# Narrow attention heads of a hybrid decoder step leave fixed filler places; filler is chained behind value transposes

## Chip, cores and metric

One core of a Trainium2 chip runs the whole program in one launch. The metric is device time in microseconds (us), from the first to the last instruction and the little around them; it is taken as the median of several runs. Engines: PE (TensorE, the matmuls), PEld (its weight loads), DVE (VectorE), ACT (ScalarE), POOL (GpSimd), SP (the queue that issues most DMAs).

## What is computed

One step of a decoder with two layers, for a prompt of 1024 tokens and for 8 sample tokens that each have 512 past tokens in a paged cache. Everything is float32 at the interface.

```python
def _diff_attn(q1, q2, q_pos, k1, k2, v, k_pos, table, lam):
    def probs(q, k):
        s = jnp.einsum('bqhd,bkhd->bhqk', q, k).astype(jnp.float32) * scale + bias
        return jax.nn.softmax(jnp.where(mask, s, NEG), axis=-1)
    p = probs(q1, k1) - lam * probs(q2, k2)
    return jnp.einsum('bhqk,bkhe->bqhe', p.astype(v.dtype), v)
...
for layer in range(DEPTH):
    h = _rmsnorm(x, norm_mix[layer])
    # even layer: 4 heads of _diff_attn and 4 of HGRN2; odd layer: 8 heads of _fox_attn and 4 of mLSTM
    x = x + y
    h = _rmsnorm(x, norm_mlp[layer])
    x = x + jnp.square(jax.nn.relu(h @ w_up[layer])) @ w_down[layer]
```

`_fox_attn` is causal attention with one softmax for each head and a forget bias in place of the relative-position bias. In this document "diff" is the attention of layer 0 and "fox" that of layer 1.

## The kernel before

Activations lie transposed (features on partitions, tokens along the free axis). The tokens are cut into two halves: half 0 holds 512 tokens, half 1 the other 512 and the 8 samples. Every projection and MLP matmul splits both operands into two float32r parts and adds three products (high by high, high by low, low by high). `wsplit` (L100 to L109) loads a block of weights and splits it: a DMA on SP, a copy on ACT (L107), a subtraction on POOL (L108). `mm3_parts` (L126) issues the matmuls, all of them on L141, 24 for each split block of the up projection.

The order of the work: projections of layer 0 and HGRN2 of half 0; diff heads of half 0 (here **narrow**: at most 512 keys); diff heads of half 1 (**wide**: up to 1024 keys); HGRN2 of half 1 with the samples' recurrence and attention; then the same for layer 1 with fox heads and mLSTM. Dense work that depends on nothing at hand is **filler**: Python generators in `self.fill` (projections that are still due, then `half` (L1410): the output projection and the MLP of a half that is ready). `tick(n)` (L184) adds rate times n to a credit and takes pieces of filler from the generators until it is used up; a piece of 4096 columns is one unit. `half` first does the part that needs no attention, then says "wait" until the heads of its half are in `heads_done`. At the end of each layer `drain("fill")` issues all that is left.

All four stages of attention run through `attend` (L592). It gets groups (two blocks of 128 query rows) and pipelines them by hand: while the transposes (`prob_t`, L654) and the value matmuls (`pv`, L669) of one group are issued, the scores (L586, L589) of the group 1 or 2 ahead are put between them, with a `tick` at each pair of key blocks. While `attend` runs, `self.chain` is true, and `mm3_parts` ties each piece of filler behind `self.after`, the last score, transpose or value matmul (L140: `issue_after`); so filler keeps the place where it was written. Elsewhere the framework's scheduler (a list scheduler that orders by readiness) puts filler where it sees fit.

For one group: score matmuls into a PSUM tile S; a minimum and the bias on DVE (L632, L634), exp on ACT (L636), the factors and the sum of two maps on DVE (L725, L727); transposes of the probabilities on PE into tile pm (L654); the split into a high part on ACT (L642, Ph) and a low part on DVE (L643, Pl); the value matmuls (L669) into po. The values themselves are transposed on PE and split on ACT and DVE, in chunks of four 128-blocks: `diff_values` (L692, L694, L695) and `fox_values` (L1263, L1267, L1268); each chunk ends with `tick(0.8)`. Wide stages have one PSUM tile pm and two S, narrow ones two pm and three S.

In the sample attention (`diff_sample` L858, `fox_sample` L1341) the probability of the sample's own token goes through DRAM: POOL writes it to `ps_a` or `ps_c`, `sample_out` (L906) reads it back on POOL's queue (L914, L912) into tile pse, multiplies it on DVE (L915) by the own value and adds it to the page values.

```python
    def diff_values(self, vt, u, hd, ps):
...
            nc.vector.tensor_tensor(Vl[:, c0:c0 + 4, :], p3, raw(Vh[:, c0:c0 + 4, :]), op=ALU.subtract)
            self.tick(0.8)
```

Of the kernel before, what the change touches and what calls it, by code (L numbers as in the profile page):

```python
# [19 lines left out]
NP = 1024  # L20
# [44 lines left out]
class Step:  # L65
# [526 lines left out]
    def attend(self, groups, depth, lead, gap):  # L592
# [91 lines left out]
    def diff_values(self, vt, u, hd, ps):  # L684
        nc = self.nc
        n = 4 * (u + 1)
        Vh = hd.tile([128, n, 128], F32R, name="Vh", tag="Vh", bufs=2)
        Vl = hd.tile([128, n, 128], F32R, name="Vl", tag="Vl", bufs=2)
        for c0 in range(0, n, 4):
            pt = ps.tile([128, 512], F32, name="pm", tag="m")  # L690
            for c in range(4):
                nc.tensor.transpose(pt[:, 128 * c:128 * c + 128], vt[:, 128 * (c0 + c):128 * (c0 + c + 1)], self.ident[:])  # L692
# [3 lines left out]
            self.tick(0.8)  # L696
        return Vh, Vl

    def diff_half(self, u, hd, pm, pS, need=()):

        nc = self.nc
        W = 512 * (u + 1)
        parts, vt, V, po, P, es, st = {}, {}, {}, {}, {}, {}, {}

        def prep(h, g):
            if g == 2 * u:
                if need:
                    self.drain("fill", need[h])
                parts[h] = self.diff_parts(h, u, hd)
                if h == 0:  # L710
                    vt[0] = self.values(self.O["va"][0:128, :], u, hd)

        def score(h, i, m):
# [5 lines left out]
            es[m] = hd.tile([128, W], F32, name="e", tag="e", bufs=5 if u else 7)  # L719
# [10 lines left out]
        def tr(h, g, j):  # L730
            if h == j == 0 and g == 2 * u:
                V[0] = self.diff_values(vt[0], u, hd, pm)
            if g == 2 * u and j == 0:
                po[h] = pm.tile([128, 512], F32, name="po", tag="po", bufs=1)
                if h < 3 and not need:
# [7 lines left out]
        def end(h, g):  # L743
            if g == 2 * u:
                if h < 3:
                    if need:
                        vt[h + 1] = self.values(self.O["va"][128 * h + 128:128 * h + 256, :], u, hd)
# [5 lines left out]
            self.tick(2.5 if u else 1.5)  # L753

        groups = []
        for h in range(4):
            for g in (2 * u, 2 * u + 1):
                steps = [lambda h=h, i=i, m=m: score(h, i, m) for i in (2 * g, 2 * g + 1) for m in range(2)]
                groups.append(Group(lambda h=h, g=g: prep(h, g), steps, g + 1, lambda j, h=h, g=g: tr(h, g, j),
                                    lambda j, p, h=h, g=g: pv(h, g, j, p), lambda h=h, g=g: end(h, g), late=u == 1 and g == 2))  # L760
        self.attend(groups, 1 if u else 2, 0 if u else 1, 1.3 if u else 1.0)
# [96 lines left out]
    def diff_sample(self, ph, ps, pS):  # L858
# [47 lines left out]
    def sample_out(self, ph, ov, pself, vs):  # L906
# [6 lines left out]
        else:  # L913
            nc.gpsimd.dma_start(pb[:], pself)  # L914
        nc.vector.tensor_tensor(pb[:], pb[:], vs[:], op=ALU.mult)  # L915
# [339 lines left out]
    def fox_values(self, vt, u, hd, ps):  # L1255
# [4 lines left out]
        for c0 in range(0, n, 4):  # L1260
            pt = ps.tile([128, 512], F32, name="pm", tag="m")
            for c in range(4):
                nc.tensor.transpose(pt[:, 128 * c:128 * c + 128], vt[:, 128 * (c0 + c):128 * (c0 + c + 1)], self.ident[:])  # L1263
# [5 lines left out]
            self.tick(0.8)  # L1269
        return VV  # L1270

    def fox_half(self, u, hd, pm, pS):

        nc, W = self.nc, 512 * (u + 1)
        self.Q2 = [hd.tile([128, 512], F32R, name=f"Q2{r}") for r in range(2)]
        self.K2 = [hd.tile([128, W], F32R, name=f"K2{r}") for r in range(2)]
        for r in range(2):
            nc.gpsimd.memset(raw(self.K2[r][64:128, :]), 0.0)
            nc.gpsimd.memset(raw(self.Q2[r][64:128, :]), 0.0)
            nc.gpsimd.memset(raw(self.Q2[r][64:66, :]), 1.0)  # L1280
# [3 lines left out]
        def prep(h, g):  # L1284
            if g == 2 * u:
# [4 lines left out]
        def score(h, qi):  # L1290
# [3 lines left out]
            e = hd.tile([128, W], F32, name="e", tag="e", bufs=4 if u else 6)  # L1294
# [8 lines left out]
        def tr(h, g, j):  # L1303
            i, r = divmod(h, 2)
            if h == j == 0 and g == 2 * u:
                VV[0] = self.fox_values(vt[0], u, hd, pm)
            if g == 2 * u and j == 0:
# [9 lines left out]
        def end(h, g):  # L1317
            i, r = divmod(h, 2)
            if g == 2 * u + 1:
# [9 lines left out]
        for h in range(8):  # L1329
            for g in (2 * u, 2 * u + 1):  # L1330
                groups.append(Group(lambda h=h, g=g: prep(h, g), [lambda h=h, qi=qi: score(h, qi) for qi in (2 * g, 2 * g + 1)], g + 1,
                                    lambda j, h=h, g=g: tr(h, g, j), lambda j, p, h=h, g=g: pv(h, g, j, p), lambda h=h, g=g: end(h, g)))
        self.attend(groups, 1 if u else 2, 1, 1.3 if u else 1.0)
# [459 lines left out]
```

## Time and profile before

| | |
|---|---|
| runs | 2935.47, 2938.91, 2945.58 us; median 2938.91 us |
| profiled execution | 2948.05 us, span of its instructions 2946.3 us |
| busy | PE 94%, DVE 47%, POOL 39%, ACT 35% of the span |
| granted clock of PE, mean | 0.97 of full |
| stages by the trace | narrow diff 325 to 470 us, wide diff 470 to 640, narrow fox 1232 to 1346, wide fox 1930 to 2200 |

"Idle" is time in which an engine runs nothing; the profile names what ended it (the releaser). [...] Lines are those of the kernel before.

### The profile page before, as it was taken

Reading aid. Unit: us, or ns where it says so; the run is one execution under the profiler, and the core shown is the slowest. Engines: PE = TensorE matmul, PEld = TensorE weight load, DVE = VectorE, ACT = ScalarE, POOL = GpSimd, SP = SyncE. Lnnn points to the kernel's source line nnn. Section 1 sums busy time; section 2 is a strip of 40 time slices with the busy share of each in tenths; the row PEclk is TensorE's granted clock in tenths of the full one; section 3 lists DMA queues with packets and bytes.
Section 4 is the critical chain, followed back from the end, with each engine's and each line's share of the span. In section 5 each row is a group of like instructions: output and inputs, shape, how many; then the busy total and the mean of one; then the engine's idle time right before and its main releaser. Section 6 shows DMA issues by size and latency. Waiting matters only on the chain. (4 is left out here: it accounts for less than half of the span.)

```text
span 2946.3 us, 44581 instructions
## 1 busy us (share of the span) xinstructions
PE 2772.6 (94%) x17410; PEld 2458.7 (83%) x17410; DVE 1375.5 (47%) x2668; ACT 1039.1 (35%) x1741; POOL 1141.5 (39%) x688
## 2 busy tenths in 40 slices
PE   8999898889889989989999989889999999999997
PEld 7999786677678878889999979867777777999997
DVE  5134457665654354374322246365544533532234
ACT  4111346552222232374323332155542223323233
POOL 3323323223843434422344434843323334344443
PEclk9999899899999999999999999989999999999998
DMA  4332444225544354523322244742235333422222
GB/s 141 112 122 80 135 152 128 76 85 163 157 125 151 110 153 151 159 78 111 120 93 88 93 152 129 235 129 85 69 111 164 107 97 103 147 94 91 90 94 73
DMA packets 174685, 349.73 MB, mean 119 GB/s; under 512 B 28914, under 2 KB 67298, under 8 KB 174474
## 3 DMA queue, kind: packets, MB, share of 16 engines
q1 hardware_dynamic: 174250, 346.81, 37.5%
q8 instruction: 137, 2.24, 0.3%
q0 software_dynamic: 224, 0.07, 0.2%
q14 instruction: 74, 0.61, 0.1%
HBM read 297.92 MB, written 48.88 MB: 118 GB/s over the span
## 5 line engine op out<-in xcount | busy, mean ns | idle before, releaser
L108 POOL TENSOR_TENSOR wl<-wr,wh 128x1024 fp32r<-128x1024 f32 (+1 forms) x361 | 866.9, 2402 | 1334.4 <-ACT wh L107 1259.8
L107 ACT ACTIVATE wh<-wr 128x1024 fp32r<-128x1024 f32 (+1 forms) x361 | 381.5, 1057 | 1126.8 <-PE acc L141 908.1
L141 PE MATMUL acc<-uh,wh 128*128 128x260 f32 (+1 forms) x2080 | 674.3, 327 | 25.6 <-DVE ul L1408 10.6
L141 PE MATMUL acc<-ul,wh 128*128 128x260 f32 (+1 forms) x2080 | 666.4, 321 | 3.8 <-DVE ul L1408 2.8
L141 PE MATMUL acc<-xh,wh 128*128 128x260 f32 (+1 forms) x1760 | 590.3, 335 | 15.7 <-ACT xh L238 7.7
L141 PE MATMUL acc<-uh,wl 128*128 128x260 f32 (+1 forms) x1856 | 602.0, 325 | 0.0
L141 PE MATMUL acc<-xl,wh 128*128 128x260 f32 (+1 forms) x1760 | 588.0, 334 | 2.7 <-DVE xl L239 2.6
L141 PE MATMUL acc<-xh,wl 128*128 128x260 f32 (+1 forms) x1760 | 586.1, 333 | 1.1 <-POOL wl L108 1.1
L141 PEld LDWEIGHTS acc<-uh,wh 128*128 128x128 f32 x2080 | 395.4, 191 | 61.1 <-DVE x L1431 10.9
L1431 DVE TENSOR_TENSOR x<-acc,x 128x260 f32<-128x260 f32 (+1 forms) x464 | 238.0, 517 | 402.7 <-PE acc L141 400.8
L141 PEld LDWEIGHTS acc<-ul,wh 128*128 128x128 f32 x2080 | 397.6, 191 | 32.6 <-DVE ul L1408 5.8
L141 PEld LDWEIGHTS acc<-uh,wl 128*128 128x128 f32 x1856 | 354.1, 191 | 28.7 <-issue 0.8
L141 PEld LDWEIGHTS acc<-xh,wh 128*128 128x128 f32 x1760 | 334.3, 190 | 50.8 <-ACT xh L238 8.0
L141 PEld LDWEIGHTS acc<-xl,wh 128*128 128x128 f32 x1760 | 334.8, 190 | 33.3 <-DVE xl L239 3.8
L141 PEld LDWEIGHTS acc<-xh,wl 128*128 128x128 f32 x1760 | 334.8, 190 | 31.6 <-POOL wl L108 1.2
L1405 DVE SCALAR_TENSOR_TENSOR acc<-acc,rb 128x260 f32<-128x260 f32 (+1 forms) x192 | 100.2, 524 | 258.5 <-PE acc L141 257.1
L141 PE MATMUL acc<-ih,wh 128*128 128x260 f32 (+2 forms) x600 | 194.0, 324 | 7.7 <-ACT wh L107 4.8
L141 PE MATMUL acc<-ih,wl 128*128 128x260 f32 (+2 forms) x600 | 192.9, 324 | 4.5 <-POOL wl L108 4.5
L141 PE MATMUL acc<-il,wh 128*128 128x260 f32 (+2 forms) x600 | 192.7, 321 | 0.0
L215 DVE TENSOR_TENSOR z<-acc,rb 128x512 f32<-128x512 f32 (+1 forms) x138 | 69.6, 511 | 259.0 <-PE acc L141 238.2
L1408 DVE TENSOR_TENSOR ul<-acc,uh 128x260 fp32r<-128x260 f32 (+1 forms) x192 | 98.5, 513 | 141.9 <-ACT uh L1407 141.4
L141 PE MATMUL acc<-x,wh 128*128 128x260 f32 x448 | 128.4, 289 | 0.8 <-DVE z L215 0.7
(406 smaller groups left out, 3826.1 us busy)
## 6 DMA issues: line engine op xcount, KB each, us to landing
wr<-in_w_up SPq DMA_DIRECT2D x128, 512.0 KB
wr<-in_w_down SPq DMA_DIRECT2D x128, 512.0 KB
wr<-in_w_in_o SPq DMA_DIRECT2D x48, 512.0 KB
wr<-in_w_out SPq DMA_DIRECT2D x32, 512.0 KB
wr<-in_w_in_e SPq DMA_DIRECT2D x27, 512.0 KB
qd<-qS SPq DMA_DIRECT2D x64, 128.0 KB
dk<-in_cache_k_a SPq DMA_DIRECT2D x32, 256.0 KB
dk<-in_cache_v_a SPq DMA_DIRECT2D x32, 256.0 KB
```

Of the source, the lines that this page charges most:

```text
L107: nc.scalar.activation(h[:, :kk, :m], r[:, :kk, :m], AF.Copy)
L108: nc.gpsimd.tensor_tensor(l[:, :kk, :m], r[:, :kk, :m], raw(h[:, :kk, :m]), op=ALU.subtract)
L141: nc.tensor.matmul(out, lhsT=w[:, k, :m], rhs=a[:, sl], start=(n == 0), stop=(n == last))
L215: nc.vector.tensor_tensor(d, p, r, op=ALU.mult)
L1405: nc.vector.scalar_tensor_tensor(p, p, 0.0, self.rb[u][:, sl], op0=ALU.max, op1=ALU.mult)
L1408: nc.vector.tensor_tensor(L[:, sl], p, raw(H[:, sl]), op=ALU.subtract)
L1431: nc.vector.tensor_tensor(x[f][:, sl], pt[:, :m], x[f][:, sl], op=ALU.add)
```

## The change

The narrow stages (half 0 of both layers) no longer go through `attend`. New functions `diff_head` and `fox_head` write one head after the other, with `self.chain` false; filler is taken by `tick(L / NP)` after each score, at rates of 5.2 and 5.0 in place of 1, and is not tied to a place. The wide stages keep `attend`, with larger ticks in its first part (5 for 4, 1.6 for 0.7). In `diff_values` and `fox_values` the transposes now set `self.after`, and a chunk's tick is 1.3 for 0.8, in the wide stages only. `half` gives up one more unit before its RMS norm. The read of the own probability is written ahead of the page values.

```diff
 def attend(...)
-        self.tick(4)
+        self.tick(5)
         for G in groups[:depth]:
             for step in G.steps:
                 step()
-                self.tick(0.7)
+                self.tick(1.6)
...
 def diff_values(...)          # fox_values the same, with L1302 for L1263
-        Vh = hd.tile([128, n, 128], F32R, name="Vh", tag="Vh", bufs=2)
+        Vh = hd.tile([128, n, 128], F32R, name="Vh", tag="Vh", bufs=u + 1)
...
-                nc.tensor.transpose(pt[:, 128 * c:128 * c + 128], vt[:, 128 * (c0 + c):128 * (c0 + c + 1)], self.ident[:])
+                self.after = nc.tensor.transpose(pt[:, 128 * c:128 * c + 128], vt[:, 128 * (c0 + c):128 * (c0 + c + 1)], self.ident[:]).ins
...
-            self.tick(0.8)
+            if self.chain:
+                self.tick(1.3)
...
+    def diff_head(self, h, hd, ps, pS, parts, nxt):
+        po = ps.tile([128, 512], F32, name="po", tag="po", bufs=1)
+        for g in range(2):
+            P = []
+            for i in (2 * g, 2 * g + 1):
+                st = hd.tile([128, 2, 2], F32, name="st", tag="st", bufs=4)
+                es = []
+                for m in range(2):
+                    S = pS.tile([128, 512], F32, name="S", tag="S")
+                    L = self.scores(S, parts[m], i)
+                    w = min(L, 256)
+                    e = hd.tile([128, 512], F32, name="e", tag="e", bufs=5)
+                    self.soft_neg(S, L, e, st[:, m, :], self.bias[:, h, 256 - w:])
+                    self.tick(L / NP)
+                    es.append(e)
+                if i == 1:
+                    after = nxt()
...
+            if g == 0:
+                Vh, Vl = self.diff_values(self.values(self.O["va"][128 * h:128 * h + 128, :], 0, hd), 0, hd, ps)
+            o = po[:, 256 * g:256 * g + 256]
+            for j in range(g + 1):
+                self.pv(o, g, j, self.prob_t(hd, ps, P, g, j), lambda kb: ((Vh[:, kb, :], 0), (Vh[:, kb, :], 1), (Vl[:, kb, :], 0)))
...
 def diff_sample(...)          # fox_sample the same
         nc.gpsimd.dma_start(pself[:].rearrange("o r -> r o"), p2[:, 512:513])
+        pb = self.own_probs(ph, pself[:].to_broadcast([128, 32]))
         pick = self.row_picker(ph)
         ov = ph.tile([128, 32], F32, name="ov", tag="ov")
         yield from self.page_values(...)
-        o = self.sample_out(ph, ov, pself[:].to_broadcast([128, 32]), self.va_s)
+        o = self.sample_out(ph, ov, pb, self.va_s)
...
 def half(...)
         if not alone:
+            yield 1
             rms()
...
 def run(...)
-                self.fill = (1, self.fill[1] + [self.half(0, 0, accM, accM)])
+                self.fill = (5.2, self.fill[1] + [self.half(0, 0, accM, accM)])
...
-                self.diff_half(0, hd, pm, pS, dp[2::3])
+                self.diff_first(hd, pm, pS, dp[2::3])
...
-                self.fill = (1, self.fill[1])
+                self.fill = ((5.0, 1)[u], self.fill[1])
...
-                    self.fox_half(u, hd, pm, pS)
+                    (self.fox_wide if u else self.fox_first)(hd, pm, pS)
```

`fox_head` is `diff_head` with one map for each row block and the normalisation on DVE or ACT; `diff_first` and `fox_first` call the heads in turn and prepare the next head's queries and keys from inside (`nxt`). Three places in the order of PE show what this moves. Names with numbers are particular buffers; K, Q are the operands of a score, vt and pm the values and the PSUM tile of a transpose, xh, xl, uh, ul and x those of filler.

The first place is PE at the start of the narrow diff heads, where head 0's first scores stand (L586, L589) and the constants of the relative-position bias (L535). Before:

```order
L286 MATMUL hms<-hsq,ones 128x512
L141 MATMUL acc<-uh,wh 128x260
L141 MATMUL acc<-x_186,wl 128x260
L586 MATMUL S<-K_3217,Q_3216 128x128
L589 MATMUL S<-K_3220,Q_3216 128x128
...
L141 MATMUL acc<-x_238,wl 128x260
L535 MATMUL pm<-oh,tb 128x384 x4
L586 MATMUL S<-K_3230,Q_3229 128x256
L589 MATMUL S<-K_3233,Q_3229 128x256
```

And now, at the same place:

```order
L286 MATMUL hms<-hsq,ones 128x512
...
L141 MATMUL acc<-xh_156,wl 128x512
L586 MATMUL S<-K_3217,Q_3216 128x128
L589 MATMUL S<-K_3220,Q_3216 128x128
L141 MATMUL acc<-xh_169,wh 128x512
...
L535 MATMUL pm<-oh,tb 128x384
L141 MATMUL acc<-ul,wh 128x260
L141 MATMUL acc<-x_225,wl 128x260
L141 MATMUL acc<-x_238,wh 128x260
L535 MATMUL pm<-oh,tb 128x384
```

The first scores stand 42 filler matmuls later (36 of 260 columns, 6 of 512), and the four L535, which stood together, have filler between them.

The second place is PE in the wide diff heads, at the second chunk of the third head's values (L692) and the first transposes of probabilities behind it (L654). Before:

```order
L586 MATMUL S<-K_5447,Q_5446 128x384
L589 MATMUL S<-K_5450,Q_5446 128x384
L692 MATMUL pm<-ident,vt 128x128 x4
L654 MATMUL pm<-ident,e 128x128 x4
L141 MATMUL acc<-xh_4690,wh 128x512
L141 MATMUL acc<-xl_4691,wh 128x512
```

Now:

```order
L586 MATMUL S<-K_5532,Q_5531 128x384
L589 MATMUL S<-K_5535,Q_5531 128x384
L692 MATMUL pm<-ident,vt 128x128 x4
L141 MATMUL acc<-uh,wh 128x512
...
L141 MATMUL acc<-uh,wl 128x512
L586 MATMUL S<-K_5545,Q_5544 128x512
L589 MATMUL S<-K_5548,Q_5544 128x512
L586 MATMUL S<-K_5545,Q_5544 128x384
L589 MATMUL S<-K_5548,Q_5544 128x384
L654 MATMUL pm<-ident,e 128x128 x4
```

Twelve filler matmuls and four of scores now stand between L692 and L654, where nothing stood.

The third place is PE at the end of the narrow diff heads: the last head's values (L692), transposes and value matmuls (L669). Now:

```order
L141 MATMUL acc<-uh,wl 128x512
L692 MATMUL pm<-ident,vt 128x128 x4
L654 MATMUL pm<-ident,e 128x128 x7
L669 MATMUL po<-Ph,Vh 128x256
...
L669 MATMUL po<-Pl,Vh 128x256
L654 MATMUL pm<-ident,e 128x128 x3
L669 MATMUL po<-Ph,Vh 128x256 x2
L669 MATMUL po<-Ph,Vl 128x256 x2
L669 MATMUL po<-Pl,Vh 128x256 x2
```

Before, the last head's transposes were:

```order
L286 MATMUL hms<-hsq,ones 128x512
L654 MATMUL pm<-ident,e 128x128 x3
L141 MATMUL acc<-uh,wh 128x512
...
L654 MATMUL pm<-ident,e 128x128 x4
L141 MATMUL acc<-uh,wh 128x512
...
L654 MATMUL pm<-ident,e 128x128 x3
L141 MATMUL acc<-uh,wh 128x512
```

So 32 matmuls of one head now stand in a row; before, 6 to 12 filler matmuls stood behind each of its three groups of transposes.

## Rows read from the trace of the kernel before

**Rows 1.** The page's first line

```profile
span 2946.3 us, 44581 instructions
```

**Rows 2.** Windows by stage: us, busy PE, PEld, DVE, ACT, POOL (instructions), PEclk, DMA share, GB/s

```profile
325.00:470.00 145.00, 129.60 (x719) 108.60 (x718) 78.68 (x205) 68.43 (x151) 43.78 (x34) 0.93 0.50 155
470.00:640.00 170.00, 140.53 (x673) 114.68 (x671) 127.69 (x230) 103.24 (x168) 46.51 (x22) 0.91 0.28 81
1232.00:1346.00 114.00, 102.14 (x752) 96.95 (x752) 87.12 (x192) 80.72 (x189) 33.83 (x23) 0.94 0.39 108
1440.00:1730.00 290.00, 284.07 (x2348) 281.97 (x2346) 95.98 (x209) 95.14 (x161) 117.14 (x49) 1.00 0.32 103
1930.00:2200.00 270.00, 244.39 (x1265) 204.22 (x1263) 159.44 (x245) 147.41 (x248) 86.28 (x46) 0.95 0.30 88
```

**Rows 3.** Waits of PE in 325 to 470 us: us in total, times, longest

```profile
PE S L586 <- ACT e L636: 3.7, 4, 2.0
PE pm L535 <- POOL tb L533: 3.0, 2, 2.6
PE S L586 <- ACT K L563: 2.2, 1, 2.2
PE S L589 <- POOL K L567: 1.3, 2, 1.0
PE pm L535 <- POOL bt L538: 1.0, 1, 1.0
```

**Rows 4.** Waits of PE in 1232 to 1346 us

```profile
PE po L669 <- DVE ft L1322: 4.2, 2, 2.1
PE acc L261 <- DVE sq L251: 2.3, 1, 2.3
```

**Rows 5.** Waits of PE in 470 to 640 us

```profile
PE S L586 <- ACT e L636: 9.3, 11, 3.4
PE pm L654 <- DVE Vl L695: 8.1, 3, 3.3
PE pm L654 <- DVE e L727: 3.2, 1, 3.2
PE po L669 <- DVE Pl L643: 2.6, 3, 1.2
```

**Rows 6.** Waits of PE in 1930 to 2200 us

```profile
PE S L586 <- ACT e L636: 6.8, 4, 4.4
PE pm L654 <- DVE VV L1268: 6.2, 4, 1.9
PE pm L1263 <- DVE VV L1268: 3.7, 2, 2.1
```

**Rows 7.** Windows of line L141 alone: us, PE busy (instructions), PEld, PEclk

```profile
940.00:1040.00 100.00, 97.12 (x411) 76.91 (x411) 1.00 0.39 125
1450.00:1700.00 250.00, 247.39 (x2054) 246.32 (x2053) 1.00 0.27 91
```

**Rows 8.** Timeline of PE, wide diff heads: start, us, what, count, idle before and its releaser

```profile
573.68 0.66 PE L654 MATMUL pm<-ident,e 128*128 128x128 f32 x4 [2.71 <-DVE Vl L695]
...
598.78 0.50 PE L586 MATMUL S<-K,Q 128*128 128x512 f32 x1 [3.41 <-ACT e L636]
```

**Rows 9.** Timeline of POOL, DVE and PE, 846 to 861 us

```profile
852.17 0.57 POOL L914 DMA_DIRECT2D pse<-ps_a  x1 [5.04 <-DMA ps_a<-dp]
...
858.52 0.91 DVE L915 TENSOR_TENSOR pse<-pse,va_s 128x32 f32<-128x32 f32 x1 [8.55 <-DMA pse<-ps_a]
...
860.08 0.79 PE L141 MATMUL acc<-xh,wh 128*128 128x512 f32 x1 [4.84 <-DVE x L1431]
```

**Rows 10.** Timeline of DVE and POOL, 801 to 812 us, and POOL's weight split (part 5)

```profile
801.77 10.42 DVE L394 TENSOR_TENSOR hq<-hq,hpe 128x256 f32<-128x256 f32 x1
...
801.75 4.67 POOL L108 TENSOR_TENSOR wl<-wr,wh 128x1024 fp32r<-128x1024 f32 x2
...
L108 POOL TENSOR_TENSOR wl<-wr,wh 128x1024 fp32r<-128x1024 f32 (+1 forms) x361 | 866.9, 2402 | 1334.4 <-ACT wh L107 1259.8
```

More of the change, by code (lines that the diff above doesn't have):

```diff
@@ L703, in diff_half, with diff_wide @@
+    def diff_wide(self, hd, pm, pS):
+        nc = self.nc
+        W, u = NP, 1
         parts, vt, V, po, P, es, st = {}, {}, {}, {}, {}, {}, {}
         def prep(h, g):
-            if g == 2 * u:
-                if need:
-                    self.drain("fill", need[h])
+            if g == 2:
                 parts[h] = self.diff_parts(h, u, hd)
@@ L1268, in fox_values @@
                 nc.vector.tensor_tensor(d[:, :, 64:128], p3[:, :, 64 * r:64 * r + 64], raw(d[:, :, 0:64]), op=ALU.subtract)
-            self.tick(0.8)
-        return VV
[L1272 to L1280, printed above, removed]
+            if self.chain:
+                self.tick(1.3)
@@ new lines, in fox_values, with fox_head @@
+        return VV
+    def fox_head(self, h, hd, ps, pS, parts, VV, nxt):
+        nc = self.nc
+        i, r = divmod(h, 2)
+        po = ps.tile([128, 512], F32, name="po", tag="po", bufs=1)
+        for g in range(2):
+            if g % 2:
+                after = nxt()
+            P = []
+            for qi in (2 * g, 2 * g + 1):
+                st = hd.tile([128, 2], F32, name="st", tag="st", bufs=4)
+                S = pS.tile([128, 512], F32, name="S", tag="S")
+                L = self.scores(S, parts, qi, mask=True)
+                e = hd.tile([128, 512], F32, name="e", tag="e", bufs=4)
+                self.soft_neg(S, L, e, st)
+                self.tick(L / NP)
+                nc.vector.reciprocal(st[:, 1:2], st[:, 1:2])
+                if r:
+                    nc.scalar.activation(e[:, :L], e[:, :L], AF.Copy, scale=st[:, 1:2])
+                else:
+                    nc.vector.tensor_scalar(e[:, :L], e[:, :L], st[:, 1:2], None, op0=ALU.mult)
+                P.append(e)
+            if h == g == 0:
+                VV = self.fox_values(self.values(self.O["vc"][0:128, :], 0, hd), 0, hd, ps)
+            o = po[:, 256 * g:256 * g + 256]
+            for j in range(g + 1):
+                self.pv(o, g, j, self.prob_t(hd, ps, P, g, j), lambda kb: ((VV[r][:, kb, :], 0), (VV[r][:, kb, :], 1)))
+        t = hd.tile([64, 512], F32, name="ft", tag="ft", bufs=1)
+        nc.scalar.copy(t[:], po[64:128, :])
+        nc.vector.tensor_tensor(t[:], po[0:64, :], t[:], op=ALU.add)
+        nc.sync.dma_start(self.os[1][0][i][64 * r:64 * r + 64, :512], t[:])
+        if r == 1 and i < 3:
+            VV = self.fox_values(self.values(self.O["vc"][128 * i + 128:128 * i + 256, :], 0, hd), 0, hd, ps)
+        return after, VV
@@ L1376, in fox_sample @@
         nc.gpsimd.dma_start(pself[:].rearrange("h (b o) -> (h b) o", o=1), e[:, 512:513])
+        pse = pself[:].rearrange("(i r) b -> r i b", r=2)
+        pb = self.own_probs(ph, tuple(pse[r].unsqueeze(0).to_broadcast([64, 4, NS]) for r in range(2)))
         pick = self.row_picker(ph)
@@ L1387, in fox_sample @@
         yield from self.page_values(ph, ps, I["cache_v_c"], PP, sel, ov)
-        pse = pself[:].rearrange("(i r) b -> r i b", r=2)
-        o = self.sample_out(ph, ov, tuple(pse[r].unsqueeze(0).to_broadcast([64, 4, NS]) for r in range(2)), self.vc_s)
+        o = self.sample_out(ph, ov, pb, self.vc_s)
         nc.sync.dma_start(self.os[1][1][0:4][:, :, 512:].rearrange("i p b -> p i b"), o[:].rearrange("p (i b) -> p i b", b=NS))
@@ L1666, in hgrn_half, with diff_first, nxt, fox_first @@
         self.staggered([self.hgrn_unit(h, u, ph, pm, need.get(h)) for h in range(4)], lag)
+    def diff_first(self, hd, pm, pS, need):
+        def nxt(h):
+            if h == 4:
+                return None
+            self.drain("fill", need[h])
+            return self.diff_parts(h, 0, hd)
+        parts = nxt(0)
+        for h in range(4):
+            parts = self.diff_head(h, hd, pm, pS, parts, lambda: nxt(h + 1))
+    def fox_first(self, hd, pm, pS):
+        self.fox_ones(512, hd)
+        parts, VV = self.fox_parts(0, 0, hd), None
+        for h in range(8):
+            parts, VV = self.fox_head(h, hd, pm, pS, parts, VV, lambda: self.fox_parts(h + 1, 0, hd) if h < 7 else None)
 @with_exitstack
```

70 lines of the change are left out of this document (46 added, 24 removed).

## Prediction, made before the run

> **What bounds the kernel now.** I read the page's busy shares first: PE runs for 94% of the span [rows 1], three products for each matmul, and no other engine is busy for half of it. The time is therefore PE's work plus PE's idle time plus what it loses while the granted clock stands at its lower level. The change removes no matmul, so it can only act on the two losses.
>
> Second, the windows by stage, to see where these losses lie [rows 2]. Idle is a window's length less PE's busy time: 145 - 129.60 = 15.4 us in the narrow diff heads, 29.5 in the wide diff heads, 11.9 in the narrow fox heads, 25.6 in the wide fox heads, together 82.4 us. The clock loss is the length times (1 - PEclk): 10.2, 15.3, 6.8 and 13.5, together 45.8 us. While a layer's left-over filler is drained, in the 290 us behind the narrow fox stage, PE idles 5.9 us and stands at the upper level throughout. So the four stages that the change rewrites hold 128 us of loss, and filler issued in them or in the drain costs the same: 100/411 = 0.243 us for 512 columns, 250/2054 = 0.122 us for 260 [rows 7]. Moving filler gains nothing by itself; it gains when it stands where PE would wait.
>
> Third, PE's waits in each of the four stages, by releaser [rows 3 to 6]. The reader is to see that no single wait is large: the list is of 1 to 4 us waits on ACT's exp, on the values' split, and on POOL's constants.
>
> **The change part by part.** Counts of filler are from the two orders; durations are from the rows.
>
> *Narrow diff heads.* Filler now goes where the scheduler finds it ready, and the first scores stand behind 36 x 0.122 + 6 x 0.243 = 5.9 us more of it. The waits for the first key operands (2.2 and 1.3), for the bias constants tb and bt (3.0 and 1.0) and the longest one of a score for exp (2.0) are each shorter than that [rows 3]: 9.5 us go. Against it, the last head's 32 matmuls stand in a row, where filler covered each of three softmax and split chains before. Such a chain shows as 3.2 us where it is bare (transposes for DVE's e) and 2.71 or 3.3 (for Vl) [rows 5, 8]; I take one of them, 3 us, as the heads ahead still overlap. Sum **-6.5**. Bounds: -9.5 if the tail costs nothing; -0.5 if tb and bt stay (4.0) and the tail costs 5.
>
> *Narrow fox heads.* The 4.2 us for the factor ft (L1322), which sat in front of chained value matmuls, go, since 45 more pieces of filler (5.5 us) now stand in the stage; the wait for the square (2.3) belongs to `half` and stays [rows 4]. The longest stretch without filler grows from 77 to 89 attention matmuls, for which I charge 1 us. Sum **-3.2**, bounds -4.2 and 0.
>
> *Wide diff heads.* Behind a chunk's transposes there are now 12 filler matmuls, 2.9 us, and four scores. They cover the 8.1 us for Vl (three waits, longest 3.3) [rows 5, 8]. The larger tick of the first part covers the 3.2 us for e, whose wait stands near the stage's start. What is late next: the filler used there is missing elsewhere, and at two heads in place of one the first scores come in a burst that outruns exp, as in the 3.41 us wait at 598.78 [rows 8], so +3.4; the longest dry stretch grows from 42 to 50 matmuls, +2. Sum -8.1 - 3.2 + 3.4 + 2 = **-5.9**, bounds -11.3 without the penalties and -0.5 with them doubled. 76 more 512-column matmuls are used in this stage, 18.5 us; they leave the drain.
>
> *Wide fox heads.* The same cover takes the 6.2 us of transposes behind VV; the 3.7 us at L1263, where the next chunk waits for the same buffer, may grow by 2, since there is less filler between chunks; the longest wait for exp, 4.4, falls in the first part, whose ticks more than double [rows 6]. Sum -6.2 + 2 - 4.4 = **-8.6**, bounds -10.6 and -2.2.
>
> *Own probabilities.* At nothing. In the kernel before, POOL already issues this read at 852.17, right behind the write it waits for (5.04 us of idle time there), long before the line that names it would suggest. The multiply on DVE then waits 8.55 us, and PE 4.84 us behind it [rows 9]. The change writes the read ahead, but the multiply keeps its place early in DVE's order, ahead of the evictions that PE needs, so the wait stays. This is the part that may not do what it says. Bounds: -4.8 if the multiply moves, +2 if POOL, whose queue the read holds, delays the row picks behind it.
>
> *The rest.* One more yield ahead of the RMS norm and single-buffered narrow values cost nothing: the wait for the square stays, and the values' loads keep their places in SP's order, so nothing is queued behind a new wait there.
>
> *Clock.* Idle time goes down by 6.5 + 3.2 + 5.9 + 8.6 = 24.2 us. In these stages clock loss is 45.8/82.4 = 0.56 of the idle time [rows 2]. Were it to follow, 13.5 us would go too; not every gap is followed by a stretch at the lower level, so I take half, **-6.7**, with bounds 0 and, at the largest idle gain, 0.56 x 35.6 = 19.9.
>
> *Sum.* 24.2 + 6.7 = 30.9 us off the profiled execution's 2948.05, whose span is 2946.3: 2917.2. The median of the runs shown is 9.1 below that execution, so **2908 us**. All bounds at their best: 35.6 + 19.9 off, 2883; all at their worst: 3.2 off, 2936.
>
> **The rivals.**
>
> *More than forecast.* One subtraction of 256 elements on DVE took 10.42 us, with POOL's weight splits running back to back from the same moment [rows 10]. If the moved filler shifts POOL's splits, this stall may not recur, up to 10.4 us, and the rest of the proportional clock gain comes with it: 2908 - 10.4 - 6.7 = 2891. For it: it is an accident of order, and the order changes. Against: other splits can fall on other DVE work.
>
> *Less than forecast.* The filler moved into attention brings its splits along. 76 and 42 more matmuls of 24 per block are 5 splits on POOL of 2402 ns each [rows 10], 12 us beside DVE's softmax chains. If those are held up by as much and the clock gains nothing, 2908 + 12 + 6.7 = 2927. For it: the same row, which shows DVE held by POOL. Against: most of DVE's softmax reads PSUM, and the mean POOL load of these stages is 27 to 32%. [...]
>
> *Slower.* The narrow heads lose their hand pipelining. If the scheduler lets the first softmax chain of each of the 12 narrow heads stand bare, at 3.2 us [rows 5], that is 38 us, with half the clock's share (0.28 x 38 = 11) 49: 2908 + 49 = 2957. It decides from 10 of the 12 heads on (10 x 4.1 = 41). For it: the dry stretches above, and single-buffered values. Against: the new order puts the next head's scores ahead of the last value matmuls of the one before, mostly with a dozen pieces of filler between.
>
> **How the numbers follow.** About 0.3%, 8.8 us, is what a measurement of this kernel can tell from no change: faster is below 2930.1, slower above 2947.7. The forecast (2896 to 2922) has 0.50, the larger gain 0.14, the smaller gain (2917 to 2938) 0.22, of which half lies below 2930.1, the slower case 0.14. Faster is 0.50 + 0.14 + 0.11 = 0.75, same 0.11, slower 0.14. The range 2883 to 2938 leaves out the slower case and a little of the larger gain.
>
> **What would show it.** Right: PE's waits at L654 for Vl and VV fall below 3 us in each wide stage; the waits for ft, tb and K in the narrow stages are gone; PE is idle under 60 us in the four stages, with PEclk up in all four; the drains are shorter by about 20 us in layer 0; DVE still waits 8 us for pse. Wrong: a new wait of PE for DVE's e or ACT's exp at the start of most narrow heads (the slower case), DVE operations of 5 us or more beside POOL's splits in the wide stages (the smaller gain), or an unchanged PEclk with fewer gaps, which would say that the clock hangs on something other than these waits.

## The result and the profile after

| | before | after |
|---|---|---|
| median of the runs, us | 2940.31 (5 runs, 2935.47 to 2951.26) | 2909.83 (5 runs, 2906.02 to 2919.53) |
| ratio, 95% interval | | 0.9898 [0.9869, 0.9927] |
| profiled execution, us | 2948.05 | 2906.02 |

The kernel became 1.0% faster, 30 us, at 2909.83 us; the forecast was 2908 us. The page of the profile after begins:

```profile
span 2904.3 us, 44586 instructions
...
PE 2757.2 (95%) x17408; PEld 2447.8 (84%) x17410; DVE 1378.9 (47%) x2668; ACT 1038.7 (36%) x1741; POOL 1142.4 (39%) x688
```

PE idles 2904.3 - 2757.2 = 147.1 us, where the profiled execution before had 173.7 (2946.3 - 2772.6). The windows by stage, which answer to [rows 2] (narrow diff, wide diff, narrow fox, the drain behind it, wide fox; same columns; each stage begins and ends where it does before, counted from its first and last scores):

```profile
330.00:460.00 130.00, 120.49 (x695) 101.64 (x694) 83.59 (x204) 68.35 (x150) 44.16 (x34) 0.99 0.54 167
460.00:643.00 183.00, 154.64 (x748) 126.46 (x746) 137.53 (x236) 108.82 (x177) 54.40 (x24) 0.93 0.27 82
1205.00:1319.00 114.00, 102.73 (x800) 98.97 (x799) 89.07 (x198) 80.67 (x191) 37.97 (x26) 0.97 0.39 116
1410.00:1700.00 290.00, 284.52 (x2352) 282.43 (x2350) 96.18 (x209) 94.69 (x161) 118.26 (x54) 1.00 0.33 107
1898.00:2168.00 270.00, 249.89 (x1311) 208.72 (x1311) 160.82 (x247) 150.00 (x250) 90.44 (x48) 0.97 0.31 92
```

Idle time of the four attention stages is 9.5 + 28.4 + 11.3 + 20.1 = 69.3 us (82.4 before) and their clock loss 1.3 + 12.8 + 3.4 + 8.1 = 25.6 us (45.8 before). The wide diff stage is longer because more filler lies in it. PEclk is the mean granted clock of a stretch, as a share of full; the traces of the two kernels show two levels of it, 1.00 (470 to 490 us in the kernel before) and 0.50 (492 to 500). PE's waits in the narrow diff heads ([rows 3] before):

```profile
PE pm L654 <- DVE hrs L291: 2.0, 1, 2.0
...
PE po L669 <- ACT Ph L642: 1.1, 1, 1.1
PE pm L535 <- POOL tb L533: 1.0, 1, 1.0
```

In the narrow fox heads ([rows 4] before):

```profile
PE acc L141 <- DVE x L1512: 4.0, 4, 1.6
PE po L669 <- DVE ft L1341: 3.1, 1, 3.1
PE acc L141 <- DVE ul L1480: 1.6, 1, 1.6
```

In the wide diff heads ([rows 5] before):

```profile
PE S L586 <- ACT e L636: 11.8, 9, 3.6
PE po L669 <- DVE Pl L643: 5.6, 2, 5.3
PE acc L141 <- DVE x L1512: 2.8, 1, 2.8
...
PE pm L654 <- DVE Vl L695: 0.6, 1, 0.6
```

And in the wide fox heads ([rows 6] before; VV is now on L1307, the values' transposes on L1302):

```profile
PE pm L654 <- DVE VV L1307: 8.4, 2, 6.3
PE po L669 <- DVE Pl L643: 3.5, 7, 1.0
PE pm L1302 <- DVE VV L1307: 2.6, 2, 1.6
...
PE S L586 <- ACT e L636: 0.2, 1, 0.2
```

The reader is to see what went as planned (K, most of tb, Vl, exp in the wide fox heads) and the two waits of over 5 us that are new, for Pl (5.3) and for VV (6.3).

### The profile page after: what moved, and what is told of

Read it like the earlier page. It is cut to its first block, busy times and chain, and to the rows that moved or that the text cites. A ratio compares the mean times of both kernels' runs of the same rounds, so it can differ in the third digit from the quotient of the medians.

```text
span 2904.3 us, 44586 instructions
## 1 busy us (share of the span) xinstructions
PE 2757.2 (95%) x17408; PEld 2447.8 (84%) x17410; DVE 1378.9 (47%) x2668; ACT 1038.7 (36%) x1741; POOL 1142.4 (39%) x688
## 5 line engine op out<-in xcount | busy, mean ns | idle before, releaser
L141 PE MATMUL acc<-uh,wh 128*128 128x260 f32 (+1 forms) x2080 | 673.5, 327 | 27.7 <-DVE x L1512 16.0
L141 PE MATMUL acc<-ul,wh 128*128 128x260 f32 (+1 forms) x2080 | 665.5, 321 | 5.9 <-DVE ul L1480 4.6
L141 PE MATMUL acc<-uh,wl 128*128 128x260 f32 (+1 forms) x1856 | 601.5, 325 | 0.0
L141 PE MATMUL acc<-xh,wh 128*128 128x260 f32 (+1 forms) x1760 | 587.3, 334 | 11.4 <-ACT xh L238 8.1
L141 PE MATMUL acc<-xl,wh 128*128 128x260 f32 (+1 forms) x1760 | 585.7, 333 | 2.5 <-DVE xl L239 2.5
L141 PE MATMUL acc<-xh,wl 128*128 128x260 f32 (+1 forms) x1760 | 583.3, 332 | 0.0
L141 PEld LDWEIGHTS acc<-uh,wh 128*128 128x128 f32 x2080 | 394.5, 191 | 67.0 <-DVE x L1512 19.6
L141 PEld LDWEIGHTS acc<-ul,wh 128*128 128x128 f32 x2080 | 396.4, 191 | 36.6 <-DVE ul L1480 7.4
L141 PEld LDWEIGHTS acc<-uh,wl 128*128 128x128 f32 x1856 | 353.4, 190 | 28.4 <-issue 0.7
L141 PEld LDWEIGHTS acc<-xh,wh 128*128 128x128 f32 x1760 | 332.8, 189 | 44.6 <-ACT xh L238 8.1
L141 PEld LDWEIGHTS acc<-xl,wh 128*128 128x128 f32 x1760 | 333.6, 190 | 31.9 <-DVE xl L239 3.4
L141 PEld LDWEIGHTS acc<-xh,wl 128*128 128x128 f32 x1760 | 333.1, 189 | 30.2 <-issue 0.8
L141 PE MATMUL acc<-ih,wh 128*128 128x260 f32 (+2 forms) x600 | 194.8, 325 | 7.3 <-ACT wh L107 5.5
L141 PE MATMUL acc<-ih,wl 128*128 128x260 f32 (+2 forms) x600 | 193.3, 324 | 4.5 <-POOL wl L108 4.5
L141 PE MATMUL acc<-il,wh 128*128 128x260 f32 (+2 forms) x600 | 193.7, 323 | 0.0
L141 PE MATMUL acc<-x,wh 128*128 128x260 f32 x448 | 128.6, 290 | 0.8 <-DVE z L215 0.7
```

Source lines behind the costliest of these rows:

```text
L141: nc.tensor.matmul(out, lhsT=w[:, k, :m], rhs=a[:, sl], start=(n == 0), stop=(n == last))
```

## The experiments

All are compared with the kernel before, run on the same chip beside them. Besides the median, the table splits the time in two, over all executions: **clock loss** is the span times (1 - its mean granted clock), **the rest** is the span without it, which is PE's work at a PEclk of 1.00 plus its idle time. PE's work does not change: in the 14 profiled executions, one of each kernel and a second of the kernel before, the rest less PE's idle time comes to 2680 to 2690 us. So differences of the rest are, to a few us, differences of idle time. The row "before" holds all executions on the three chips of the experiments; by chip its rest is 2852, 2853 and 2851 us and its clock loss 89, 87 and 90. The rest varies little from one execution to the next (standard deviation 1 to 4 us; 7 for f1_kdve_hq).

| kernel | executions | median us | ratio, 95% interval | rest us | clock loss us |
|---|---|---|---|---|---|
| before | 57 | 2940 to 2942 | | 2852 | 89 |
| after | 5 | 2909.83 | 0.9898 [0.9869, 0.9927] | 2831 | 79 |
| e1_narrow | 12 | 2943.03 | 1.0002 [0.9984, 1.0020] | 2841 | 100 |
| e2_wide | 6 | 2918.01 | 0.9916 [0.9888, 0.9944] | 2836 | 80 |
| e3_small | 12 | 2953.28 | 1.0043 [1.0026, 1.0060] | 2853 | 101 |
| e4_hq_pool | 12 | 2940.50 | 0.9983 [0.9964, 1.0001] | 2846 | 91 |
| e5_no_small | 6 | 2909.41 | 0.9894 [0.9873, 0.9914] | 2828 | 81 |
| e6_ticks | 6 | 2922.18 | 0.9935 [0.9920, 0.9950] | 2833 | 88 |
| e7_values | 12 | 2939.27 | 0.9995 [0.9979, 1.0010] | 2847 | 93 |
| e8_kdve | 5 | 2905.89 | 0.9882 [0.9863, 0.9901] | 2828 | 76 |
| f1_kdve_hq | 6 | 2911.28 | 0.9891 [0.9870, 0.9911] | 2828 | 82 |
| f2_spread | 4 | 2907.91 | 0.9876 [0.9856, 0.9896] | 2828 | 80 |
| f3_all | 5 | 2891.94 | 0.9824 [0.9807, 0.9840] | 2814 | 76 |

**e1_narrow**: only the narrow heads are new. Against the changed kernel:

```diff
-        self.tick(5)
+        self.tick(4)
...
-                self.tick(1.6)
+                self.tick(0.7)
...
-                self.after = nc.tensor.transpose(pt[:, 128 * c:128 * c + 128], vt[:, 128 * (c0 + c):128 * (c0 + c + 1)], self.ident[:]).ins
+                nc.tensor.transpose(pt[:, 128 * c:128 * c + 128], vt[:, 128 * (c0 + c):128 * (c0 + c + 1)], self.ident[:])
...
-                self.tick(1.3)
+                self.tick(0.8)
```

and the two small edits of e3_small taken back.

> The changed kernel with its wide stages, own-probability reads and the yield ahead of the RMS norm as before: only the narrow heads are new. Theory A (the gain comes from the waits that each part takes away in its own stages): about 0.4% faster than before (2940), 2928 us (9.7 us of waits and 2.7 of clock), idle time in the wide stages as before (29.5 and 25.6). Theory B (the gain outside the four stages, at the DVE stall of 10.4 us and the wait of 4.8 us for the own probability, comes with any new order): 2915 to 2925 with those two gone from the recurrence of half 1. Theory C (narrow heads lose by giving up their pipeline): slower than 2945.

The time did not move, which none of the three theories gave. The table shows what offset what: the rest fell by 11 us, near theory A's 9.7, and the clock loss rose by 11. The windows of its profile (the four attention stages):

```profile
330.00:458.00 128.00, 121.25 (x696) 102.44 (x695) 83.66 (x203) 66.95 (x148) 42.96 (x34) 0.97 0.54 168
458.00:634.00 176.00, 146.03 (x683) 118.48 (x682) 130.12 (x231) 105.19 (x171) 48.89 (x22) 0.89 0.27 81
1216.00:1330.00 114.00, 103.60 (x798) 99.80 (x797) 90.25 (x197) 80.07 (x190) 37.31 (x23) 0.96 0.39 115
1914.00:2190.00 276.00, 246.56 (x1264) 205.51 (x1264) 158.50 (x245) 148.37 (x248) 86.48 (x46) 0.94 0.28 84
```

The narrow stages idle 6.8 and 10.4 us (15.4 and 11.9 before), so their heads lost nothing by giving up the pipeline: theory C falls. The wide stages, whose code is that of before, idle 30.0 and 29.4 us (29.5 and 25.6 before) and stand at a PEclk of 0.89 and 0.94 (0.91 and 0.95 before). But the clock loss of the four stages together, 44 us, is no larger than before (45.8). In this profile 7 us of the added loss lie elsewhere, in the recurrence of half 1 and in a stretch in which PE never idles. The window, in the kernel before and in e1_narrow:

```profile
700.00:750.00 50.00, 50.00 (x282) 40.72 (x281) 28.60 (x66) 12.19 (x20) 19.79 (x16) 1.00 0.36 111
700.00:750.00 50.00, 50.00 (x251) 40.52 (x250) 26.77 (x60) 10.53 (x19) 17.11 (x15) 0.86 0.32 101
```

PE is busy for 50.00 of 50.00 us in both, and r1_before (below), a second profile of the kernel before, has 1.00 there too. In the 5 us ahead of the fall PE runs only matmuls of the recurrence, most of them of 64 columns and of 1 (L388, L470), with no filler between them. The kernel before has 7 us of such work at 714 us and keeps its clock, so what tips it is not shown.

**e2_wide**: only the wide part, in the kernel before.

```diff
-        self.tick(4)
+        self.tick(5 if depth == 1 else 4)
...
-                self.tick(0.7)
+                self.tick(1.6 if depth == 1 else 0.7)
...
+                self.after = at if u else self.after
...
-            self.tick(0.8)
+            self.tick(1.3 if u else 0.8)
```

> The kernel before with only the wide part: larger ticks in the first part of the pipeline, and filler chained behind the value transposes, in the wide stages alone. Theory A: 2921 us, 0.6% faster (14.5 us of waits and 4 of clock); PE's waits behind Vl and VV under 3 us in each wide stage, the narrow stages as before (15.4 and 11.9 idle). Theory B: in the wide stages new waits (exp, Pl) give back what Vl and VV free, at most 7 us of idle time go there, and what else is gained lies in the recurrence of half 1.

2918 us: most of the whole change's gain, 16 us of the rest and 9 of clock loss, near theory A's 14.5 and 4. In its profile the two wide stages idle 25.5 and 20.0 us (29.5 and 25.6 before), more of a fall than theory B's 7. But not all of it is by theory A's waits: PE waits 1.8 us for Vl, and still 7.4 for VV (L1270).

**e3_small**: only the own probability's read, written earlier, and one more yield.

```diff
+        pb = self.own_probs(ph, pself[:].to_broadcast([128, 32]))
         pick = self.row_picker(ph)
...
         if not alone:
+            yield 1
             rms()
```

> The kernel before with only the own-probability read written earlier and one more yield ahead of the RMS norm. Theory A: no change, 2935 to 2945, PE still waits about 4.8 us behind the own probability. Theory B: the order of the recurrence moves and 5 to 15 us go, 2925 to 2935, in the recurrence of half 1.

0.43% slower, against both theories. The rest is unchanged (2853 against 2852), so in sum no idle time was added or taken. The whole difference is clock loss, 12 us; which of the two edits moves it was not run. The profile holds the stall of hq (9.27 us), DVE's wait for the own probability (8.52) and PE's wait for the eviction behind it (4.84), in two lines of DVE and one of PE:

```profile
812.02 9.27 DVE L394 TENSOR_TENSOR hq<-hq,hpe 128x256 f32<-128x256 f32 x1
...
868.23 0.94 DVE L921 TENSOR_TENSOR pse<-pse,va_s 128x32 f32<-128x32 f32 x1 [8.52 <-DMA pse<-ps_a]
```

```profile
869.83 0.80 PE L141 MATMUL acc<-xh,wh 128*128 128x512 f32 x1 [4.84 <-DVE x L1438]
```

**e4_hq_pool**: the product that stalled in [rows 10], on POOL.

```diff
-            nc.vector.tensor_tensor(Q[:, :, hh:], Q[:, :, hh:], p2[:, :, 0:1].to_broadcast([128, nb, hh]), op=ALU.mult)
+            nc.gpsimd.tensor_tensor(Q[:, :, hh:], Q[:, :, hh:], p2[:, :, 0:1].to_broadcast([128, nb, hh]), op=ALU.mult)
```

> The kernel before with the decayed queries of the recurrence (hq by hpe, L394) multiplied on POOL in place of DVE, so that DVE has no two-input SBUF product there that POOL's own work can hold up. If the 10.4 us stall of that one product is in every execution of the kernel before: about 10 us faster, 2930, with no idle time of PE over 5 us in 780 to 830 us. If it is an accident of the one profiled execution, or POOL's longer queue gives it back: 2935 to 2945.

The time lies in the second range, and the interval of the ratio just touches 1; the rest fell by 6 us. A stall of 10 us in every execution would have given more, if POOL's longer queue gives none of it back, which was not told apart. A second profile of the kernel before, r1_before, with nothing edited:

> The kernel before once more, for a second profile. If its idle time is set by the order of the instructions: 163 to 167 us of idle time on PE again, of it 9 to 11 in one wait behind the product hq (L394) at about 802 us, and the time differs from 2948 by as much as the clock loss differs. If the stall is an accident of one execution: no DVE operation over 5 us, idle time 150 to 155.

Its time was 2946.53 us, its PE busy for 2782.2 of 2944.8 us, so idle for 162.6, 11 less than the first. That is near the first branch's idle time, but without the stall that it names. On DVE and POOL, where the first had the 10.42 us:

```profile
804.79 1.18 DVE L394 TENSOR_TENSOR hq<-hq,hpe 128x256 f32<-128x256 f32 x1
```

```profile
803.32 4.87 POOL L108 TENSOR_TENSOR wl<-wr,wh 128x1024 fp32r<-128x1024 f32 x2
```

The same product beside two weight splits took 1.18 us; it began 1.47 us after them, and 0.02 us after them in the first profile. Of the 11 profiles with this product on DVE three hold one of over 5 us: before, e3_small and e8_kdve, which has the change. In the first profile the 48 products of this form have a median of 0.68 us, and the four that met no POOL operation took 0.41 to 0.46. So the stall belongs to some executions, not to the order alone, and the 11 us between the two profiles of the kernel before can't be counted as the change's.

**e5_no_small**: the changed kernel without the two small edits (those of e3_small taken back).

```diff
-        pb = self.own_probs(ph, pself[:].to_broadcast([128, 32]))
...
         if not alone:
-            yield 1
             rms()
```

> The changed kernel with the own-probability read and the RMS norm's place as before, so narrow and wide parts together. If the two small edits cost as much here as in the kernel before (e3_small, 11 us): 2899, 1.5% faster than before. If their cost there is tied to that kernel's order in the recurrence of half 1 (where its DVE stall of 9.3 us stands): 2910, as the changed kernel.

2909.4 us, as the changed kernel. The 12 us that they cost in the kernel before are not there in this order.

**e6_ticks** and **e7_values** part e2_wide in two. The larger ticks alone:

```diff
-        self.tick(4)
+        self.tick(5 if depth == 1 else 4)
...
-                self.tick(0.7)
+                self.tick(1.6 if depth == 1 else 0.7)
```

> The kernel before with only the larger ticks in the first part of the wide stages' pipeline (5 for 4, 1.6 for 0.7); values' filler as before. Theory A (cover where PE waited): the waits for e at the start go, 3.2 us in the wide diff heads and 4 to 6 us in the wide fox heads, with clock 10 us: 2932. Theory B (what counts is the order further on, in the recurrence of half 1, where e2_wide has no DVE stall): as e2_wide, 2918, if the stall of the product hq is gone there, and 2940 if it stands.

And the chained filler behind the values alone:

```diff
+                self.after = at if u else self.after
...
-            self.tick(0.8)
+            self.tick(1.3 if u else 0.8)
```

> The kernel before with only the filler chained behind the wide stages' value transposes, 1.3 for 0.8 units. Theory A: the waits behind Vl fall from 8.1 to under 2 us, those behind VV do not (e2_wide has 7.4), with clock 10 to 14 us: 2928 to 2932. Theory B: as e2_wide, 2918, if the stall of hq is gone, 2940 if it stands.

The ticks alone give 18 us, nearly all of it idle time (19 us of the rest); in the wide fox heads the wait for exp falls from 6.8 to 2.1 us. But these waits are the smaller part. By the profiles PE idles 15.5 us less than in r1_before (147.1 against 162.6), the four attention stages only 4.7 less (77.0 against 81.7). From the end of the wide diff heads to the start of the narrow fox heads, the stretch with the recurrence of half 1, it is 11 less (13.0 against 24.0), with no stall of hq in either. This is theory B's place, without the stall that theory B names; why the recurrence waits less was not tested. The values' filler alone gives nothing: 5 us of the rest, and 4 more of clock loss. It does what it was written for, as PE's waits in the wide diff heads of e7_values show, where no wait for Vl is left, but others took its place (Pl had 2.6 in [rows 5]):

```profile
PE S L586 <- ACT e L636: 6.9, 8, 3.4
PE pm L654 <- DVE hrs L291: 4.9, 1, 4.9
PE po L669 <- DVE Pl L643: 4.4, 3, 2.9
```

**e8_kdve**: the changed kernel with the keys' low part on DVE.

```diff
-            nc.gpsimd.tensor_tensor(K2[:], kd[:], raw(K1[:]), op=ALU.subtract)
+            nc.vector.tensor_tensor(K2[:], kd[:], raw(K1[:]), op=ALU.subtract)
...
-            nc.gpsimd.tensor_tensor(K2[0:64, :], kd[0:64, :], raw(K1[0:64, :]), op=ALU.subtract)
+            nc.vector.tensor_tensor(K2[0:64, :], kd[0:64, :], raw(K1[0:64, :]), op=ALU.subtract)
```

> The changed kernel with the low part of the attention keys (L567, L570) subtracted on DVE in place of POOL. If what is left in the wide stages comes from DVE operations that POOL's key and weight splits hold up (2.8 us each at 496 and 499 us for 0.7 us of work, behind which PE waits 5.3 us): that wait and the 6.3 us behind VV shrink, idle time of the four stages falls by 6 to 12 us and the time by 8 to 15, 2895 to 2902. If DVE itself is the limit there: 1.3 us more on DVE for each wide key, 24 in all, the waits on exp and Pl grow, 2910 to 2920.

What it was to explain stands in the changed kernel's timeline. DVE, from 496 us:

```profile
496.18 2.87 DVE L575 SCALAR_TENSOR_TENSOR Q<-qd,Q 64x512 fp32r<-64x512 f32 x1
498.98 2.85 DVE L239 SCALAR_TENSOR_TENSOR xl<-x,col,xh 128x512 fp32r<-128x512 f32 x1
...
503.43 0.73 DVE L239 SCALAR_TENSOR_TENSOR xl<-x,col,xh 128x512 fp32r<-128x512 f32 x1
...
505.17 0.66 DVE L643 TENSOR_TENSOR Pl<-pm,Ph 128x512 fp32r<-128x512 f32 x1
```

POOL in the same stretch:

```profile
495.97 2.54 POOL L567 TENSOR_TENSOR K<-kd,K 128x1024 fp32r<-128x1024 f32 x1 [5.12 <-PE acc L141]
498.46 2.83 POOL L108 TENSOR_TENSOR wl<-wr,wh 128x1024 fp32r<-128x1024 f32 x1
```

And PE:

```profile
505.88 0.80 PE L669 MATMUL po<-Pl,Vh 128*128 128x256 f32 x2 [5.29 <-DVE Pl L643]
```

Two DVE operations take a little longer than the POOL split that each meets, 2.87 and 2.85 us (0.73 for the same L239 operation at 503.43), Pl comes late behind them and behind the operations queued after them, and PE waits 5.29. With the key split gone from POOL, PE's waits for Pl in these heads are 1.2 us in all, and the idle time of the trace falls from 147.1 to 139.5 us although one product hq stalled for 11.7 us in this execution. The time, 2905.9, is 4 us below the changed kernel's, less than the two intervals can tell apart, and above the 2895 to 2902 expected. So the wait for Pl goes when the key split leaves POOL; what that is worth is not shown.

**f1_kdve_hq** joins e8_kdve and e4_hq_pool, **f2_spread** puts filler between two score steps that stand together in the pipeline, and **f3_all** joins both, with a larger tick in the wide stages' first part.

```diff
-                for _ in range(share):
+                for k in range(share):
+                    if k:
+                        self.tick(1.2)
                     todo.pop(0)()
...
-                self.tick(1.6)
+                self.tick(2.4)
```

> The changed kernel with the attention keys' low part on DVE (as e8_kdve) and the recurrence's product hq on POOL (as e4_hq_pool), so that neither the key splits nor the product can stall behind one another. If time is 2697 us plus PE's idle time plus its clock loss: idle 131 of e8_kdve less its stall of 8.4, so 122 to 125, and 2895 to 2900. If clock loss rises as idle time falls (as between the kernel before, e1_narrow and e4_hq_pool): 2904 to 2910.

> The changed kernel with 1.2 units of filler between the two score steps that stand together where a wide diff head begins. If the waits of 3.6 and 3.4 us for exp there come from that burst: both go, idle time in the wide diff heads falls by 5 to 7 us, and the time is 2900 to 2905. If the softmax chain on DVE is late anyway: the wait moves to the next transposes, 2908 to 2914.

> f1_kdve_hq and f2_spread together, and 2.4 units in place of 1.6 at each score of the wide stages' first part. If the three add up: 2885 to 2892, 1.7% faster than before. If they don't, because filler is missing elsewhere or clock loss rises: 2898 to 2905.

f1_kdve_hq missed: its profile idles 146.0 us, not 122 to 125, and with no stall of hq left it is no faster than e8_kdve. f2_spread took the two waits of over 3 us for exp (the longest is 2.8), and the wide diff heads idle 21.7 us in its profile against 28.4, as expected; but the rest fell by 3 us only, and the time, 2907.9, lies between its two ranges. f3_all, at 2891.9 us (0.9824), the upper end of its first range, beats both kernels, by 18 us against the changed one. The rest fell by 17 us, more than the others' shares (3 and 3). The larger tick was not run alone, so whether the surplus is its own or comes from the parts together is not shown. Its four windows:

```profile
331.00:460.00 129.00, 121.21 (x695) 102.59 (x694) 83.64 (x212) 65.74 (x147) 29.69 (x24) 0.98 0.55 166
460.00:655.00 195.00, 175.02 (x851) 143.15 (x851) 141.28 (x252) 114.47 (x184) 50.65 (x23) 0.96 0.30 91
1201.00:1317.00 116.00, 108.10 (x821) 102.36 (x820) 93.16 (x209) 82.20 (x191) 29.50 (x17) 0.97 0.40 116
1894.00:2164.00 270.00, 252.88 (x1330) 213.49 (x1329) 163.00 (x253) 150.73 (x251) 69.53 (x32) 0.97 0.31 91
```

The wide diff heads idle 20.0 us there, against 28.4 in the changed kernel, with 12 us more of length that filler fills.

## Why the prediction was right, step by step

**The sum.** 24.2 us of idle time and 6.7 of clock loss were forecast. Over all executions the rest fell by 2852 - 2831 = 21 us and the clock loss by 10. Sign, size and the order of the two terms were right. Between the two profiled executions the fall is larger (26.6 us of idle time), since the first holds a stall that the second profile of before doesn't have; against that one it is 162.6 - 147.1 = 15.5. Of the 24.2 only 13.1 came in the four stages that the sum is about (82.4 to 69.3; 12.4 against r1_before's 81.7); between the wide diff heads and the narrow fox heads it was 5.5 (24.0 to 18.5), which the sum had at nothing. The bounds of the sum leave out those of the own probabilities, -4.8 and +2.

**The signs.** PEclk is up in all four stages, the wait for Vl is 0.6 us, and DVE still waits 6.9 us for pse. But the wait for VV is 8.4 us, ft stands at 3.1, and the four stages idle 69.3 us, not under 60. Of the signs of being wrong none came: the longest DVE operation in the wide stages took 3.78 us. The steps below are judged by one profile on each side; two profiles of the kernel before differ by 0.3 to 1.3 us in the idle time of a stage (r1_before: 15.8, 30.1, 11.5 and 24.3).

**Narrow diff heads, -6.5:** 15.4 to 9.5, so -5.9. The waits for K went, tb fell from 3.0 to 1.0; the tail costs hrs 2.0 and Ph 1.1, the 3 us that were charged. This step held.

**Narrow fox heads, -3.2:** -0.6 in the window, within what two profiles differ by. ft came down only from 4.2 to 3.1, and filler itself now waits, 4.0 us for DVE's evictions of x and 1.6 for ul. What failed is the step that the 4.2 us for ft go because 45 more pieces of filler stand in the stage. Three of these waits, for ul (1.55 us), for x (1.15 of the 4.0) and for ft (3.09), go back to a DVE operation beside a POOL weight split; DVE and POOL at each place:

```profile
1218.62 2.75 DVE L1480 TENSOR_TENSOR ul<-ol,uh 128x520 fp32r<-128x520 f32 x1
1218.45 2.37 POOL L108 TENSOR_TENSOR wl<-wr,wh 128x1024 fp32r<-128x1024 f32 x1 [1.90 <-ACT wh L107]
...
1241.33 2.60 DVE L1332 TENSOR_SCALAR e<-e,st 128x512 f32<-128x512 f32 x1
1240.87 2.77 POOL L108 TENSOR_TENSOR wl<-wr,wh 128x1024 fp32r<-128x1024 f32 x1 [4.32 <-PE S L589]
...
1263.81 1.58 DVE L1332 TENSOR_SCALAR e<-e,st 128x256 f32<-128x256 f32 x1
1262.63 2.60 POOL L108 TENSOR_TENSOR wl<-wr,wh 128x1024 fp32r<-128x1024 f32 x1 [5.57 <-ACT wh L107]
```

The first is ul itself (0.69 us for the one before it); behind the two others the eviction of x and ft stand in DVE's queue. Each of the three DVE operations ended 0.2 to 0.6 us after the split did (L1332 takes 0.49 us for 512 columns at 1221.48). The longest wait for x, 1.55 us, stands behind DVE operations of ordinary length.

**Wide diff heads, -5.9:** -1.1 (29.5 to 28.4), no more than two profiles differ by. Vl went from 8.1 to 0.6 and e (L727) is gone, as forecast, and the wait for exp grew by 2.5 (3.4 forecast). Not in the sum was the wait for Pl of 5.3 us, behind two DVE operations that took 2.87 and 2.85 us beside POOL's key and weight splits of 2.54 and 2.83 (the rows at 496.18 and 498.98 us, e8_kdve), and 2.8 us for x; nor that the wait for the square fell from 3.4 to 0.4. The wait for Pl is what the rival "less than forecast" supposes, as in the narrow fox heads.

**Wide fox heads, -8.6:** -5.5 (25.6 to 20.1). exp fell from 6.8 to 0.2, by more than the 4.4 forecast. The step that failed is that the same cover takes the 6.2 us of transposes behind VV: it is 8.4 us now, 6.3 of it once. The cover stands there as planned, twelve filler matmuls and scores from 1914.56 to 1919.4 us. The rows of DVE and POOL say why it was too short:

```profile
1919.21 0.40 DVE L1307 TENSOR_TENSOR VV<-pm,VV 128x256 fp32r<-128x256 f32 x1
1919.54 2.23 DVE L1370 TENSOR_SCALAR e<-e,st 128x896 f32<-128x896 f32 x1
...
1922.95 2.25 DVE L251 TENSOR_TENSOR sq<-sq,sqt 128x512 f32<-128x512 f32 x1
1925.13 0.41 DVE L1307 TENSOR_TENSOR VV<-pm,VV 128x256 fp32r<-128x256 f32 x1
```

```profile
1918.93 2.35 POOL L108 TENSOR_TENSOR wl<-wr,wh 128x1024 fp32r<-128x1024 f32 x1 [5.71 <-ACT wh L107]
1922.30 2.35 POOL L570 TENSOR_TENSOR K<-kd,K 64x1024 fp32r<-64x1024 f32 x1 [1.03 <-ACT K L563]
```

The second of two VV subtractions stood 5.9 us behind the first, behind two operations that took 2.2 us each beside a POOL split (0.69 for the same L1370 operation at 2049.98 us, 0.68 for L251 at 1917.41). L1370, like L1332 above, reads one tensor and a column of factors, so it is not only products of two tensors that took longer there. ACT was late too: its copies of the two high parts, which the subtractions need, began at 1918.74 and 1920.40, 4.2 us and more after the transposes. Filler on PE covered a transpose's own chain here, but not the queues on ACT and DVE. With the key split off POOL (e8_kdve) the longest wait for VV is 3.3 us.

**Own probabilities, 0:** the step that PE's wait stays holds in e3_small and not in the changed kernel. DVE still waits, 6.9 us in layer 0 and 6.6 in layer 1; alone (e3_small) PE's wait is 4.84, the same as before. In the changed kernel PE's wait behind it is gone, and e5_no_small, with 4.0 us of it, is as fast, so its going is worth nothing that the time shows.

**Clock, -6.7:** -10, right in sign, but its rule (half of the idle time's share, everywhere) is not borne out. e1_narrow lost 11 us of idle time and gained 11 of clock loss; e3_small changed no idle time and gained 12; e6_ticks lost 19 and its clock loss stayed. The parts' idle times add up to -26 us (-11, -16 and +1), against -21 for all and -24 for narrow and wide together (e5_no_small); their clock losses add up to +14 (+11, -9 and +12), against -10. That the sum of the two terms came out so near is in part luck: the idle time forecast in the four stages fell by 13 us only, and the difference came from outside them and from the clock.

**The rivals.** The bare softmax chains of the slower case are not there (e1_narrow). The larger gain's cause, the stall of hq (a product; the prediction calls it a subtraction), is real but not in every execution, and f1_kdve_hq shows no gain without it. The smaller gain's cause, DVE held by POOL's splits, is there in three of the four stages: the operations in the rows above took 1.58 to 2.87 us beside a split, and those of the same lines and shapes 0.35 to 0.75 where POOL ran nothing. What the prediction holds against it, that most of DVE's softmax reads PSUM, agrees with the trace for Pl: all 120 of its subtractions (L643, from the PSUM tile pm) took 0.53 to 0.69 us in the changed kernel, beside POOL's operations or not. The four stages' idle time fell 11 us short of the sum; what came elsewhere made up for it.

## What to carry to other kernels

Split a time into clock loss and the rest over several executions before explaining a difference: one edit here moved only the clock (e3_small), and one moved both by the same amount in opposite ways (e1_narrow). Look for a gain outside the stage that was edited, too: most of what the larger ticks gained lay in the recurrence. Take a second profile of the kernel before, too, before counting a single long stall as a gain. When filler covers a wait of PE, look next at the queue of the engine that releases it: here that was mostly DVE, whose operations took up to 2.87 us beside a subtraction on POOL.

## What was not expected of the hardware

The same DVE product, in the same kernel and beside two POOL splits, took 10.42 us in one execution and 1.18 in another; in the first it ended only when seven POOL operations had gone by. The clock loss of a whole program moved by 11 and 12 us (e1_narrow, e3_small) with idle time down or unchanged. In e1_narrow's profile 7 us of it lie in a window of 50 us in which PE is busy throughout (PEclk 0.86, and 1.00 in the kernel before), so the clock fell there without idle time of PE in the window; what brought it on stays open.
